# Moving one top-k block to ScalarE, the memory projections to fp32 matmuls, and w_out's splits to three engines, in a hybrid decoder layer

## The chip, the cores and the metric

The kernel runs on one core of a Trainium2 chip. The core has TensorE (PE in the profile, with its weight loads as PEld), VectorE (DVE), ScalarE (ACT), GpSimd (POOL) and SyncE (SP), which here only issues transfers. The metric is the device time of one execution in microseconds.

## The reference, cut to what matters

One decoder layer over 1024 tokens of width 1024. Group A is sparse attention: an indexer scores all keys, each query keeps its 256 best, and 8 heads attend to those. Group B is dense differential attention. Both go through `w_out`. Cross attention over 256 memory tokens and a convolutional gated feed-forward follow.

```python
def dsa_attention(q, k, v, q_idx, k_idx, w_idx):
    topk = min(TOPK_MAX, S // 4)                     # 256
    def block(args):                                 # 128 queries
        logits = jnp.einsum('bqhd,bsd->bqhs', qib, k_idx)
        score = jnp.einsum('bqh,bqhs->bqs', wib, jax.nn.relu(logits)).astype(jnp.float32)
        score = jnp.where(causal[None], score, -jnp.inf)
        _, idx = lax.top_k(score, topk)
        ...

def token_mixer(hn, cos, sin, w_in, ...):
    proj = hn @ w_in
    ...
    out_a = dsa_attention(q_a, k_a, v_a, q_i, k_i, w_i).reshape(B, S, A_WIDTH)
    out_b = diff_attention(q_b, k_b, v_b, lam)
    out_b = (rms_normalize(out_b) * (1.0 - lambda_init)).reshape(B, S, B_WIDTH)
    return jnp.concatenate([out_a, out_b], axis=-1) @ w_out

def cross_attention(hn, memn, w_xq, w_xk, w_xv, w_xo, g_xq, g_xk):
    q = rmsnorm((hn @ w_xq).reshape(B, S, X_HEADS, X_HEAD_DIM), g_xq)
    k = rmsnorm((memn @ w_xk).reshape(B, M, X_HEADS, X_HEAD_DIM), g_xk)
    v = (memn @ w_xv).reshape(B, M, X_HEADS, X_HEAD_DIM)
    ...

def reference(...):
    h = h + token_mixer(rmsnorm(h, g_mix), ...)
    h = h + cross_attention(rmsnorm(h, g_xattn), rmsnorm(mem, g_mem), ...)
    h = h + conv_glu(rmsnorm(h, g_ffn), ...)
```

## The kernel before

**Split products.** A float32 product is made of three matmuls in the format fp32r (`mm3`, lines 287 to 289): high times high, high times low, low times high. So each operand exists as a high part (a copy into fp32r) and a low part (the source minus the high part). Matmuls on plain float32 operands also occur: the transposes, the products with attention weights (`a_av`, line 1016, and `b_av`, line 776) and `x_o` (line 1255).

**Weights.** `Weights` holds a list of jobs in order of use. A job loads 128 x 2 x 512 floats into a `raw` tile (line 168, on SP's queue), and `parts` writes the high part (line 181 on ACT or line 183 on POOL) and the low part (line 184, on DVE or POOL) into `wp` pages, of which there are 12. A pair such as `("a", "d")` says which engine makes the high part and which the low part; `AD`, `PD`, `AP_` are such pairs. `pump` runs the next jobs when pages are free.

**Stages.** The projections from `w_in` come first (to about 270 us of the profile), then group B (270 to 470), then group A (470 to 690), then the rest of `w_out`, cross attention and the feed-forward. Beside group B, and at the start of group A, `mem_step` spreads the projections of the memory tokens (`mem_mm`: eight units of eight `mm3`, weights `w_xk` and `w_xv`, stationary side `memT`).

**Top-k.** For the query blocks 2 to 7 the threshold of each row is found bit by bit in 32 steps (`topk_iter`). Block i has 128 x (i+1) keys. `GROUPS` says on which engine a block counts. On ACT, a step is one `Sign` over the scores with a running sum (line 532) and then two short DVE instructions (lines 534 and 536) that set the next candidate, which the next Sign needs. On DVE, a step is one scan with a count per block (line 544) and two short ones (546 and 547, or 549 and 550). `topk_mask` makes the mask at the end. `tick` hands out steps according to `PACE`, one pair of numbers for each phase (projections, group B, group A): a step per that many microseconds of estimated work. `topk_finish` runs what is left before a block is used.

**Group A.** `a_qt` splits the queries (`split_heads`, lines 436 and 437) and transposes them, `a_s` makes the scores (lines 995 and 996) and adds the mask on DVE (998), `a_t` transposes (670) with copies on ACT (661), `a_av` multiplies by the values. `a_ob` normalizes group B's output (1027 to 1031). `wout_unit` makes the first half of the product with `w_out` inside this stage.

**Order.** The program is written unit by unit, and a scheduler then decides the order on each engine. Within an engine and within a queue, instructions keep that order.

Of the kernel before, what the change touches and what calls it, by code (L numbers as in the profile page):

```python
# [9 lines left out]
F32 = mybir.dt.float32  # L10
# [8 lines left out]
P = 128  # L19
# [25 lines left out]
def hybrid_layer(ctx, tc, I, out):  # L45
# [98 lines left out]
    class Weights:  # L144
# [9 lines left out]
        def load(self):  # L154

            while self.nload < len(self.jobs) and self.jobs[self.nload][1] is None:
                self.nload += 1
            if self.nload == len(self.jobs):
                return
            _, src, n, _, kind, _ = self.jobs[self.nload]  # L160
            raw = rawt()
            if kind == "memT":
                sp.dma_start(raw.rearrange("p a (b m) -> p a b m", b=2), src)
            elif self.nload == 0:
                for j in range(2):
# [20 lines left out]
        def split(self):  # L186
            i = self.nsplit
            key, src, n, engines, kind, _ = self.jobs[i]
            while src is not None and i not in self.raws:
                self.load()  # L190
# [25 lines left out]
            elif kind == "D":  # L216
                fpart(fi["g"][:, 1, :])
            elif kind == "memT":
                for j in range(2):
                    pg = self.page(key)  # L220
                    for b in range(2):
                        v = slice(256 * b, 256 * b + 256)
                        gk = gmem[:, n + 2 * j + b:n + 2 * j + b + 1]
                        act.activation(pg[:, 0, v], raw[:, j, v], AF.Copy, scale=gk)
                        dve.scalar_tensor_tensor(pg[:, 1, v], raw[:, j, v], gk, pg[:, 0, v].bitcast(F32),
                                                 op0=OP.mult, op1=OP.subtract)
            elif kind == "xq":
# [28 lines left out]

    def add_chunk(key, w, c0, n, engines):
        for k in range(0, KT, 2):
            W.add(key, w[k * P:(k + 2) * P, c0:c0 + n].rearrange("(j p) n -> p j n", p=P), n, engines)

    XW = 'CAAA'
    offs = np.cumsum([0] + W_CHUNKS)
# [3 lines left out]
    for k in range(0, KT, 4):  # L266
        W.add("memT", I["memT"][k * P:(k + 4) * P, :].rearrange("(a b p) m -> p a b m", a=2, p=P), k, None, "memT")
    for w in ("xk", "xv"):
        for c in range(2):
            add_chunk((w, c), I["w_" + w], 512 * c, 512, {"A": (AP_, ("p", "p")), "B": (AD, AP_), "C": (AD, AD), "D": (AD, PD), "E": (AP_, AP_)}[XW[2 * (w == "xv") + c]])  # L270
    for half in range(2):
        for c in range(2):
            add_chunk(("out", half, c), I["w_out"], 512 * c, 512, (PD, PD))
    for c in range(2):
# [157 lines left out]

    def split_heads(tag, src, nh):

        hl = rt(tag, [P, nh, 2, 64], F32R, "hl")
        act.copy(hl[:, :nh, 0, :], src)
        dve.tensor_tensor(hl[:, :nh, 1, :], src, hl[:, :nh, 0, :].bitcast(F32), op=OP.subtract)
        return hl
# [69 lines left out]

    GROUPS = [(x.split("-")[0], tuple(int(y) for y in x.split("-")[1])) for x in 'act-23,dve-45,dve-67'.split(",")]
    cand = [mtile([P, 3], I32, f"cand{g}") for g in range(len(GROUPS))]  # L510
# [85 lines left out]

    PACE = [dict(zip(("act", "dve"), [float(y) for y in x.split(",")])) for x in '4,6:4.5,10:4.5,5'.split(':')]
    phase = [0]
# [247 lines left out]
    def mem_prep():  # L846
        pages = W.get("memT", 4)
        for j in range(KT):
            v = pages[j // 2][:, :, (j % 2) * 256:(j % 2) * 256 + 256]
            mstat[j] = (v[:, 0, :], v[:, 1, :])  # L850
        for t in range(2):
# [10 lines left out]
    def mem_mm(key, t, p, ks):  # L862
        pages = W.get(key, 8)
        s = slice(t * P, (t + 1) * P)
        for k in ks:
            mh, ml = mstat[k]
            mm3(p, mh[:, s], ml[:, s], pages[k][:, 0, :], pages[k][:, 1, :], k == 0, k == KT - 1)

# [106 lines left out]
    def a_qt(i, g):  # L975
        if g == 0:
            a_qs[i] = kq([P, 8, P], F32R, "qas")
        hl = split_heads("hl", a_q[i][g], 4)
        p = trp()
# [44 lines left out]
    def a_ob(i):  # L1024
        r = small("rr")
        sq = rt("t2", [P, 512], F32, "sq")
        dve.tensor_tensor(sq, ob[i], ob[i], op=OP.mult)
        dve.tensor_reduce(ssb[:, i, :], sq.rearrange("p (h d) -> p h d", h=4), axis=AX.X, op=OP.add)
        rstd(pool, r[:, 0:4], ssb[:, i, :], 4, 1.0 / 128)
        pool.tensor_scalar(r[:, 0:4], r[:, 0:4], 1.0 - LAMBDA_INIT, 1.0, op0=OP.mult, op1=OP.mult)  # L1030
        dve.tensor_tensor(a_mix[i][:, 512:1024].rearrange("p (h d) -> p h d", h=4), ob[i].rearrange("p (h d) -> p h d", h=4),
                          r[:, 0:4].unsqueeze(2).to_broadcast([P, 4, P]), op=OP.mult)
# [683 lines left out]
```

## Time and profile before

| | |
|---|---|
| three runs | 1692.95, 1697.2 and 1699.25 us; median 1697.2 |
| the profiled execution | 1697.69 us, of which its span is 1695.9 |
| busy time in the span | PE 1570.8 us (93%), DVE 1296.0 (76%), ACT 736.7 (43%), POOL 666.8 (39%) |
| weight loads of PE | 1284.2 us (76%) |
| HBM | 129 GB/s over the span |

The 1.8 us between the profiled execution's time and its span lie outside the instructions. Shares over the whole span mix stages with different limits, so the stages are to be read one by one. A busy PE includes the tail of each matmul, which overlaps the next one, so that gaps shorter than the tail don't show as idle.

### The profile page before, as it was taken

Reading aid. Unit: us, or ns where it says so; the run is one execution under the profiler, and the core shown is the slowest. Engines: PE = TensorE matmul, PEld = TensorE weight load, DVE = VectorE, ACT = ScalarE, POOL = GpSimd, SP = SyncE. Lnnn points to the kernel's source line nnn. Section 1 sums busy time; section 2 is a strip of 40 time slices with the busy share of each in tenths; the row PEclk is TensorE's granted clock in tenths of the full one; section 3 lists DMA queues with packets and bytes.
Section 4 is the critical chain, followed back from the end, with each engine's and each line's share of the span. In section 5 each row is a group of like instructions: output and inputs, shape, how many; then the busy total and the mean of one; then the engine's idle time right before and its main releaser. Section 6 shows DMA issues by size and latency. Waiting matters only on the chain.

```text
span 1695.9 us, 22395 instructions
## 1 busy us (share of the span) xinstructions
PE 1570.8 (93%) x7660; PEld 1284.2 (76%) x7660; DVE 1296.0 (76%) x2524; ACT 736.7 (43%) x1469; POOL 666.8 (39%) x908
## 2 busy tenths in 40 slices
PE   8899988878889989999999978999999999899999
PEld 7788766667778778878777766887777777778887
DVE  5736998999999987467553588999988888665554
ACT  6545576566655326325442234333333333343432
POOL 2746666545440230140100032556666566541121
PEclk9999999899989999999999989999999999999999
DMA  8321225222230212261202121555544554698812
GB/s 284 94 82 58 71 93 163 73 62 78 90 100 26 70 68 69 71 220 63 75 25 88 62 87 65 179 174 191 174 164 166 179 180 167 251 366 320 315 50 75
DMA packets 112161, 220.05 MB, mean 130 GB/s; under 512 B 18480, under 2 KB 38448, under 8 KB 112048
## 3 DMA queue, kind: packets, MB, share of 16 engines
q1 hardware_dynamic: 91072, 148.37, 26.5%
q0 software_dynamic: 18384, 61.36, 10.3%
q10 hardware_dynamic: 2592, 8.91, 1.4%
q8 instruction: 60, 0.98, 0.2%
q14 instruction: 53, 0.43, 0.1%
HBM read 160.92 MB, written 57.67 MB: 129 GB/s over the span
## 4 chain that ended last, share of the span: by engine, by line
PE 47%; DVE 31%; DMA 8%; issue 6%; POOL 5%; ACT 3%; SPq 0%; ACTq 0%; DVEq 0%; POOLq 0%
PE acc L287 8%; PE acc L288 8%; PE acc L289 8%; DVE jk L544 6%; DVE wp L184 4%; PE big L288 3%; PE big L287 3%; PE big L289 3%; DMA fs<-u_d 2%; POOL fs L1529 2%; PE trp L287 2%; PE trp L288 2%; PE trp L289 2%; PE big L1255 2%; DMA raw<-in_w_ffn_in_dram 2%
## 5 line engine op out<-in xcount | busy, mean ns | idle before, releaser
L184 DVE TENSOR_TENSOR wp<-raw,wp 128x512 fp32r<-128x512 f32 (+1 forms) x200 | 192.9, 973 | 21.8 <-ACT wp L181 13.2
L181 ACT CAST wp<-raw 128x512 fp32r<-128x512 f32 (+1 forms) x188 | 110.1, 614 | 173.3 <-DVE raw L206 121.4
L1580 DVE TENSOR_TENSOR wp<-fo,wp 128x1024 fp32r<-128x1024 f32 x77 | 100.6, 1322 | 76.8 <-ACT wp L1579 75.2
L1529 POOL TENSOR_TENSOR fs<-fs,fs 128x512 f32<-128x512 f32 x88 | 126.8, 1441 | 77.6 <-DMA fs<-u_d 56.8
L1579 ACT CAST wp<-fo 128x1024 fp32r<-128x1024 f32 x77 | 79.8, 1049 | 108.9 <-PE big L289 47.0
L287 PE MATMUL acc<-wp,xh 128*128 128x512 f32 (+1 forms) x272 | 110.3, 407 | 9.4 <-ACT X L625 9.4
L183 POOL TENSOR_SCALAR wp<-raw 128x512 fp32r<-128x512 f32 (+1 forms) x64 | 46.7, 740 | 177.5 <-DVE rst L110 63.4
L289 PE MATMUL acc<-wp,xl 128*128 128x512 f32 (+1 forms) x272 | 109.8, 404 | 0.0
L288 PE MATMUL acc<-wp,xh 128*128 128x512 f32 (+1 forms) x272 | 109.5, 404 | 0.0
L661 ACT COPY pt<-trp 128x512 f32<-128x512 f32 (+3 forms) x144 | 65.6, 476 | 69.0 <-PE trp L670 68.5
L184 POOL TENSOR_TENSOR wp<-raw,wp 128x512 fp32r<-128x512 f32 x52 | 69.2, 1349 | 45.7 <-ACT wp L181 45.6
L1016 PEld LDWEIGHTS acc<-va_t,pt 128*128 128x128 f32 x576 | 74.0, 195 | 7.1 <-ACT pt L661 5.0
L1016 PE MATMUL acc<-va_t,pt 128*128 128x65 f32 x576 | 76.6, 273 | 2.6 <-ACT pt L661 2.0
L1626 POOL TENSOR_TENSOR hr<-hr,r 128x512 f32<-128x512 f32 x16 | 26.9, 1692 | 123.0 <-DMA fo<-ws_d 59.6
L1061 POOL DMA_DIRECT2D h_d<-xr x16 | 9.3, 579 | 165.6 <-DVE xr L1060 147.3
L999 ACT ACTIVATE ea<-ea,sta 128x128 f32<-128x128 f32 (+7 forms) x64 | 49.3, 777 | 49.8 <-DVE sta L998 46.4
L287 PEld LDWEIGHTS acc<-wp,xh 128*128 128x128 f32 x272 | 53.0, 195 | 23.0 <-ACT X L625 11.6
L544 DVE TENSOR_SCALAR_CACHE_REDUCE jk<-mb,cx 128x640 bf16<-128x640 uint16 (+1 forms) x64 | 68.6, 1072 | 0.7
L1482 POOL TENSOR_TENSOR fg<-fc,fg 128x1024 f32<-128x1024 f32 x21 | 50.9, 2425 | 36.3 <-ACT fc L1477 36.1
L544 DVE TENSOR_SCALAR_CACHE_REDUCE jk<-mb,cand 128x640 bf16<-128x640 bf16 (+3 forms) x60 | 64.4, 1073 | 0.4
L288 PE MATMUL acc<-wp,wp 128*128 128x512 f32 x152 | 61.2, 403 | 2.8 <-DVE wp L184 2.8
L1474 ACT ACTIVATE fc<-fa,cw 128x1024 f32<-128x1024 f32 x22 | 27.4, 1245 | 81.9 <-DVE fa L1433 72.2
(419 smaller groups left out, 5140.6 us busy)
## 6 DMA issues: line engine op xcount, KB each, us to landing
raw<-in_w_ffn_in_dram SPq DMA_DIRECT2D x44, 512.0 KB, 4.2
fs<-in_w_ffn_out_dram POOLq DMA_DIRECT2D x44, 256.0 KB, 3.8
ws_d<-fs POOLq DMA_DIRECT2D x44, 256.0 KB, 2.3
fs<-u_d POOLq DMA_DIRECT2D x44, 256.0 KB, 3.8
us_d<-fs POOLq DMA_DIRECT2D x44, 256.0 KB, 2.9
fo<-us_d SPq DMA_DIRECT2D x44, 256.0 KB, 5.3
fo<-ws_d SPq DMA_DIRECT2D x44, 256.0 KB, 5.4
u_d<-fg POOLq DMA_DIRECT2D x21, 512.0 KB, 4.4
```

The costliest lines, as they stand in the source:

```text
L181: act.copy(pg[:, 0, :n], src)
L184: (dve if el == "d" else pool).tensor_tensor(pg[:, 1, :n], src, pg[:, 0, :n].bitcast(F32), op=OP.subtract)
L287: pe.matmul(o, lhsT=lh, rhs=rh, start=start, stop=False)
L288: pe.matmul(o, lhsT=lh, rhs=rl, start=False, stop=False)
L289: pe.matmul(o, lhsT=ll, rhs=rh, start=False, stop=stop)
L544: dve.tensor_scalar(jk[:, :n], src, th[:, j:j + 1], None, op0=OP.is_ge, op1=OP.add, accum_out=cnt[:, j:j + 1])
L661: act.copy(dst, src)
L1016: pe.matmul(acc[:, hh * 65:hh * 65 + 65], lhsT=pt, rhs=va_t[:, kt, :], start=kt == 0, stop=kt == i)
L1482: pool.tensor_tensor(g, cv, g, op=OP.mult)
L1529: pool.tensor_tensor(o, p, q, op=op)
L1579: act.copy(hi, raw)
L1580: dve.tensor_tensor(lo, raw, hi.bitcast(F32), op=OP.subtract)
```

## The change

1. **Top-k.** Block 6 (896 keys) counts on ACT instead of DVE; block 7 stays on DVE alone. The paces become 7 and 12 in group B (from 4.5 and 10) and 4 and 4.5 in group A (from 4.5 and 5).
2. **Memory projections.** `memT` is stored once, scaled, as plain float32; `w_xk` and `w_xv` are loaded straight into a page ("direct"), with no split; each `mm3` becomes one float32 matmul. A chunk takes 4 pages instead of 8.
3. **w_out.** The first chunk's low parts are made on POOL (its high parts on POOL and ACT); in the other three chunks half of the high parts move from POOL to ACT, and the low parts stay on DVE.
4. **Group A.** The low part of the queries (line 437) and the scaling of group B's output (line 1031) move from DVE to POOL, the square (line 1027) from DVE to ACT.

```diff
@@ load / split
-            while self.nload < len(self.jobs) and self.jobs[self.nload][1] is None:
+            while self.nload < len(self.jobs) and (self.jobs[self.nload][1] is None or self.jobs[self.nload][4] == "direct"):
...
             elif kind == "memT":
+                pg = self.page(key).bitcast(F32)
                 for j in range(2):
-                    pg = self.page(key)
                     for b in range(2):
...
-                        act.activation(pg[:, 0, v], raw[:, j, v], AF.Copy, scale=gk)
-                        dve.scalar_tensor_tensor(pg[:, 1, v], raw[:, j, v], gk, pg[:, 0, v].bitcast(F32),
-                                                 op0=OP.mult, op1=OP.subtract)
+                        act.activation(pg[:, j, v], raw[:, j, v], AF.Copy, scale=gk)
+            elif kind == "direct":
+                sp.dma_start(self.page(key).bitcast(F32), src)
@@ jobs
-    XW = 'CAAA'
...
-            add_chunk((w, c), I["w_" + w], 512 * c, 512, {"A": (AP_, ("p", "p")), "B": (AD, AP_), "C": (AD, AD), "D": (AD, PD), "E": (AP_, AP_)}[XW[2 * (w == "xv") + c]])
+            add_chunk((w, c), I["w_" + w], 512 * c, 512, None, "direct", 1)
...
-            add_chunk(("out", half, c), I["w_out"], 512 * c, 512, (PD, PD))
+            add_chunk(("out", half, c), I["w_out"], 512 * c, 512, (("p", "p"), AP_) if half + c == 0 else (PD, AD))
@@ top-k
-    GROUPS = [(x.split("-")[0], tuple(int(y) for y in x.split("-")[1])) for x in 'act-23,dve-45,dve-67'.split(",")]
+    GROUPS = [(x.split("-")[0], tuple(int(y) for y in x.split("-")[1])) for x in 'act-23,act-6,dve-45,dve-7'.split(",")]
-    PACE = [dict(zip(("act", "dve"), [float(y) for y in x.split(",")])) for x in '4,6:4.5,10:4.5,5'.split(':')]
+    PACE = [dict(zip(("act", "dve"), [float(y) for y in x.split(",")])) for x in '4,6:7,12:4,4.5'.split(':')]
@@ mem_mm
-        pages = W.get(key, 8)
+        pages = W.get(key, 4)
...
-            mh, ml = mstat[k]
-            mm3(p, mh[:, s], ml[:, s], pages[k][:, 0, :], pages[k][:, 1, :], k == 0, k == KT - 1)
+            pe.matmul(p, lhsT=mstat[k][:, s], rhs=pages[k // 2].bitcast(F32)[:, k % 2, :], start=k == 0, stop=k == KT - 1)
@@ a_qt, a_ob
-        hl = split_heads("hl", a_q[i][g], 4)
+        hl = split_heads("hl", a_q[i][g], 4, pool)
...
-        dve.tensor_tensor(sq, ob[i], ob[i], op=OP.mult)
+        act.activation(sq, ob[i], AF.Square)
...
-        dve.tensor_tensor(a_mix[i][:, 512:1024].rearrange("p (h d) -> p h d", h=4), ob[i].rearrange("p (h d) -> p h d", h=4),
+        pool.tensor_tensor(a_mix[i][:, 512:1024].rearrange("p (h d) -> p h d", h=4), ob[i].rearrange("p (h d) -> p h d", h=4),
```

Three places show how rows move. The first is ACT's order early in group B, before the change: `e` are the exponentials of group B, `pt` and `qbs` the copies that PE's next matmuls read.

```order
347 L889 COPY kt_3310<-trp_3305 128x512
348 L876 ACTIVATE sq_3315<-X_3313 128x512
349 L755 ACTIVATE e_3377,st_3371<-e_3377,st_3371 128x256 x2
350 L777 ACTIVATE ob_2733<-acc_3143,st_3166 128x128
351 L727 CAST qbs_3363<-trp_3360 128x256
352 L661 COPY pt_3369<-trp_3365 128x384
353 L727 CAST qbs_3435<-trp_3432 128x256
354 L755 ACTIVATE e_3462,st_3451<-e_3462,st_3451 128x896
```

The same place with the change (the line numbers are those of the changed file, one to three lower); `mb_940` is the Sign of block 6, and `cand_522` the candidate that it waits for.

```order
333 L531 ACTIVATE mb_940,ccnt_526<-sc_941,cand_522 128x896
334 L754 ACTIVATE e_3331,st_3325<-e_3331,st_3325 128x256
335 L886 COPY kt_3264<-trp_3259 128x512
336 L873 ACTIVATE sq_3269<-X_3267 128x512
337 L754 ACTIVATE e_3331,st_3325<-e_3331,st_3325 128x256
338 L776 ACTIVATE ob_2719<-acc_3097,st_3120 128x128
339 L726 CAST qbs_3317<-trp_3314 128x256
340 L531 ACTIVATE mb_940,ccnt_526<-sc_941,cand_522 128x896
341 L660 COPY pt_3323<-trp_3319 128x384
342 L726 CAST qbs_3357<-trp_3354 128x256
343 L754 ACTIVATE e_3384,st_3373<-e_3384,st_3373 128x896
```

A Sign now stands among group B's copies about once a unit: 22 of its 32 steps lie beside group B and 10 beside group A.

The second place is DVE's order early in group A (block 2), before the change: `jk` are the scans of the blocks 6 (128x896) and 7 (128x1024), `ea` the masked scores.

```order
950 L546 TENSOR_SCALAR crej_529<-ccnt_526 128x2
951 L1031 TENSOR_TENSOR mixt_5274<-ob_2731,rr_5405 128x512
952 L547 SCALAR_TENSOR_TENSOR cand_523<-crej_529,cand_523 128x2
953 L1020 RECIPROCAL sta_5232<-acc_5275 128x4
954 L544 TENSOR_SCALAR jk_5241,ccnt_526<-mb_936,cand_523 128x896
955 L1021 TENSOR_TENSOR mixt_5274<-acc_5275,sta_5232 128x256
956 L437 TENSOR_TENSOR hl_5559<-qat_5494,hl_5559 128x4x64
957 L544 TENSOR_SCALAR jk_5243,ccnt_526<-mb_938,cand_523 128x1024
```

The same place with the change:

```order
942 L543 TENSOR_SCALAR jk_5090,ccnt_528<-mb_942,cand_524 128x1024
943 L995 ISA ea_5103,sta_5063<-big_5100,mb_932,ra 128x384
944 L995 ISA sta_5063 128x1
945 L545 TENSOR_SCALAR crej_532<-ccnt_528 128x1
946 L533 TENSOR_SCALAR crej_530<-ccnt_526 128x1
947 L546 SCALAR_TENSOR_TENSOR cand_524<-crej_532,cand_524 128x1
948 L535 SCALAR_TENSOR_TENSOR cand_522<-crej_530,cand_522 128x1
949 L995 ISA ea_5133,sta_5063<-big_5130,mb_932,ra 128x384
```

The scans of block 6 and the rows of lines 1031 and 437 are gone from DVE; two short rows a step (533 and 535) stay behind for block 6. Of the 32 scans of block 6, 4 stood beside group B and 28 beside group A; of block 7's, 4 and 28 before, 1 and 31 now.

The third place is SP's queue just ahead of group B, before the change: `qa_d` are stores of the last projection, `raw` weight loads, `vb` and `mtok` what group B and the memory norm read first.

```order
82 L654 DMA qa_d<-X_2483 128x512
83 L654 DMA qa_d<-X_2542 128x512
84 L168 DMA raw_2682<-in_w_xk_dram 128x2x512
85 L691 DMA vb_2741<-vb_d 128x8x128
86 L853 DMA mtok_2743<-in_mem_dram 128x1024
87 L853 DMA mtok_2747<-in_mem_dram 128x1024
88 L168 DMA raw_2788<-in_w_xk_dram 128x2x512
```

With the change:

```order
87 L226 DMA wp_2879<-in_w_xk_dram 128x2x512
88 L653 DMA qa_d<-X_2540 128x512
89 L226 DMA wp_2955<-in_w_xk_dram 128x2x512
90 L226 DMA wp_3033<-in_w_xk_dram 128x2x512
91 L226 DMA wp_3095<-in_w_xk_dram 128x2x512
92 L226 DMA wp_3157<-in_w_xv_dram 128x2x512
93 L690 DMA vb_2727<-vb_d 128x8x128
94 L851 DMA mtok_2729<-in_mem_dram 128x1024
```

Between the store of `qa_d` and `vb` four weight loads of 512 KB now stand where one stood. A direct load writes into a page, so it waits for the last matmul that read the page before.

## Rows read from the trace of the kernel before

**Rows 1.** Busy time by stage (PE, PEld, DVE, ACT, POOL), granted clock, DMA share, GB/s.

```profile
165.00:270.00 105.00, 95.58 (x399) 75.45 (x398) 100.33 (x284) 71.51 (x173) 69.13 (x105) 0.97 0.24 80
270.00:470.00 200.00, 161.56 (x940) 134.75 (x938) 190.51 (x469) 125.82 (x310) 103.18 (x171) 0.93 0.31 95
470.00:690.00 220.00, 199.08 (x1316) 174.06 (x1316) 193.76 (x442) 106.30 (x202) 42.14 (x114) 0.97 0.21 68
650.00:690.00 40.00, 38.99 (x308) 36.54 (x307) 21.93 (x40) 28.37 (x43) 0.00 (x0) 1.00 0.14 47
270.00:300.00 30.00, 22.96 (x104) 16.42 (x103) 28.96 (x70) 20.17 (x45) 19.69 (x43) 0.89 0.67 207
```

**Rows 2.** Chain that ended last, by line, in 270 to 470, then 470 to 690.

```profile
by line: DVE e L753 12.6%; DVE e L765 9.9%; DVE jk L544 8.0%; PE acc L776 7.6%; issue 5.4%; ACT e L755 4.2%; DVE st L764 3.5%; PE acc L287 2.8%; PE acc L288 2.7%; DVE wp L184 2.7%; PE acc L289 2.7%; DVE sc L584 2.5%; DVE kb L705 2.5%; PE tr
by line: DVE jk L544 25.0%; DVE ea L998 11.5%; PE acc L1016 8.5%; issue 8.3%; PE trp L670 5.1%; DVE wp L184 5.0%; PE big L995 2.6%; DVE mx L1042 2.5%; PE big L996 2.3%; DVE sc L584 1.9%; DMA h_d<-xr 1.8%; DVE hl L437 1.8%; DVE xr L1060 1.7%
```

**Rows 3.** PE's timeline: start, length, line; two stretches, in cross attention.

```profile
821.12 3.59 PE L1255 MATMUL big<-ptx,vx 128*128 128x512 f32 x8
824.55 0.60 PE L1245 MATMUL trp<-ident,ex 128*128 128x128 f32 x4
...
949.75 0.39 PE L287 MATMUL acc<-wp,oxh 128*128 128x512 f32 x1
...
950.43 0.39 PE L287 MATMUL acc<-wp,oxh 128*128 128x512 f32 x1
```

**Rows 4.** DVE's groups in 270 to 470: count, busy us, mean ns, idle before.

```profile
L184 DVE TENSOR_TENSOR wp<-raw,wp 128x512 fp32r<-128x512 f32 x8 | 6.4, 817 | 0.0
L544 DVE TENSOR_SCALAR_CACHE_REDUCE jk<-mb,cand 128x896 bf16<-128x896 bf16 x3 | 3.4, 1140 | 0.0
L764 DVE SCALAR_TENSOR_TENSOR st<-st,neglam 128x1 f32<-128x1 f32 x32 | 10.8, 344 | 0.2
```

**Rows 5.** Line 764 over the span: shortest, median and longest ns.

```profile
L764 DVE SCALAR_TENSOR_TENSOR st<-st,neglam x32: 196/217/1337, 291.0 to 463.2; 128x1 f32<-128x1 f32 x32
```

**Rows 6.** DVE's groups in 470 to 690, shapes apart where they differ.

```profile
L544 DVE TENSOR_SCALAR_CACHE_REDUCE jk<-mb,cx 128x1024 bf16<-128x1024 uint16 x16 | 20.4, 1275 | 0.3
L544 DVE TENSOR_SCALAR_CACHE_REDUCE jk<-mb,cx 128x896 bf16<-128x896 uint16 x16 | 18.2, 1139 | 0.3
L184 DVE TENSOR_TENSOR wp<-raw,wp 128x512 fp32r<-128x512 f32 x28 | 20.0, 739 | 0.8 <-POOL wp L183 0.8
L437 DVE TENSOR_TENSOR hl<-qat,hl 128x256 fp32r<-128x256 f32 x14 | 5.8, 419 | 0.0
L1031 DVE TENSOR_TENSOR mixt<-ob,rr 128x512 f32<-128x512 f32 x8 | 5.5, 690 | 0.0
L546 DVE TENSOR_SCALAR crej<-ccnt 128x2 int32<-128x2 f32 x13 | 2.5, 196 | 0.1
L547 DVE SCALAR_TENSOR_TENSOR cand<-crej,cand 128x2 int32<-128x2 int32 x13 | 2.0, 156 | 0.1
L544 DVE DVE_READ_ACCUMULATOR jk<-mb,cx 128x1 f32 x32 | 2.6, 82 | 0.0
```

**Rows 7.** ACT in group B: two rows of its timeline, and its splits in 270 to 470.

```profile
296.37 1.05 ACT L755 ACTIVATE e<-e,st 128x896 f32<-128x896 f32 x1 [1.40 <-DVE st L753]
...
297.41 0.36 ACT L727 CAST qbs<-trp 128x256 fp32r<-128x256 f32 x1
...
L181 ACT CAST wp<-raw 128x512 fp32r<-128x512 f32 x17 | 10.2, 618 | 7.8 <-DMA raw<-in_w_xk_dram 4.1 <-DMA raw<-in_w_xv_dram 1.7 <-POOL wp L184 0.8
```

**Rows 8.** What the Signs of the blocks 2 and 3 (line 532) waited for: us, times.

```profile
  DVE cand L536: 24.3, 18
```

**Rows 9.** POOL's low parts in 270 to 470.

```profile
L184 POOL TENSOR_TENSOR wp<-raw,wp 128x512 fp32r<-128x512 f32 x24 | 32.5, 1369 | 5.1 <-ACT wp L181 5.0
```

**Rows 10.** Waits: PE in 470 to 690, POOL in 270 to 470: us, times, longest.

```profile
PE big L995 <- DVE sta L998: 7.4, 10, 1.1
...
POOL hl L717 <- DMA qt<-qk_d: 3.9, 2, 2.6
```

More of the change, by code (lines that the diff above doesn't have):

```diff
@@ L188, in split @@
             key, src, n, engines, kind, _ = self.jobs[i]
-            while src is not None and i not in self.raws:
+            while src is not None and kind != "direct" and i not in self.raws:
                 self.load()
@@ L255, in hybrid_layer, with add_chunk @@
     W = Weights()
-    def add_chunk(key, w, c0, n, engines):
+    def add_chunk(key, w, c0, n, engines, kind="std", npages=2):
         for k in range(0, KT, 2):
-            W.add(key, w[k * P:(k + 2) * P, c0:c0 + n].rearrange("(j p) n -> p j n", p=P), n, engines)
-    XW = 'CAAA'
+            W.add(key, w[k * P:(k + 2) * P, c0:c0 + n].rearrange("(j p) n -> p j n", p=P), n, engines, kind, npages)
     offs = np.cumsum([0] + W_CHUNKS)
@@ L266, in hybrid_layer @@
     for k in range(0, KT, 4):
-        W.add("memT", I["memT"][k * P:(k + 4) * P, :].rearrange("(a b p) m -> p a b m", a=2, p=P), k, None, "memT")
+        W.add("memT", I["memT"][k * P:(k + 4) * P, :].rearrange("(a b p) m -> p a b m", a=2, p=P), k, None, "memT", 1)
     for w in ("xk", "xv"):
         for c in range(2):
-            add_chunk((w, c), I["w_" + w], 512 * c, 512, {"A": (AP_, ("p", "p")), "B": (AD, AP_), "C": (AD, AD), "D": (AD, PD), "E": (AP_, AP_)}[XW[2 * (w == "xv") + c]])
+            add_chunk((w, c), I["w_" + w], 512 * c, 512, None, "direct", 1)
     for half in range(2):
         for c in range(2):
-            add_chunk(("out", half, c), I["w_out"], 512 * c, 512, (PD, PD))
+            add_chunk(("out", half, c), I["w_out"], 512 * c, 512, (("p", "p"), AP_) if half + c == 0 else (PD, AD))
     for c in range(2):
@@ L431, in rope, with split_heads @@
         dve.tensor_tensor(x, x, ctab, op=OP.mult)
-    def split_heads(tag, src, nh):
+    def split_heads(tag, src, nh, eng=None):
         hl = rt(tag, [P, nh, 2, 64], F32R, "hl")
         act.copy(hl[:, :nh, 0, :], src)
-        dve.tensor_tensor(hl[:, :nh, 1, :], src, hl[:, :nh, 0, :].bitcast(F32), op=OP.subtract)
+        (eng or dve).tensor_tensor(hl[:, :nh, 1, :], src, hl[:, :nh, 0, :].bitcast(F32), op=OP.subtract)
         return hl
@@ L846, in mem_prep @@
     def mem_prep():
-        pages = W.get("memT", 4)
+        pages = W.get("memT", 2)
         for j in range(KT):
-            v = pages[j // 2][:, :, (j % 2) * 256:(j % 2) * 256 + 256]
-            mstat[j] = (v[:, 0, :], v[:, 1, :])
+            mstat[j] = pages[j // 4].bitcast(F32)[:, j % 4 // 2, (j % 2) * 256:(j % 2) * 256 + 256]
         for t in range(2):
@@ L916, in mem_unit @@
         if t == 1:
-            W.free(8)
+            W.free(4)
             if (w_, c) == ("xv", 1):
-                W.free(4)
+                W.free(2)
         if w_ == "xk":
```

## The prediction

> **What bounds the kernel now.** I read busy time by stage first, since shares over the whole span hide which engine limits where [rows 1]. Beside group B (270 to 470 us) DVE is busy 190.5 of 200 us, beside group A (470 to 690) 193.8 of 220; PE is busy 161.6 and 199.1. At the end of group A (650 to 690), where top-k is over, DVE falls to 21.9 of 40 us and PE rises to 39.0 of 40, at full clock. The reader is to see there that the same group A work runs on a full PE as soon as DVE has room. The chain of waits says the same [rows 2]: beside group A the top-k scans (line 544) alone hold 25.0% of it (55 us), the masked scores on DVE (998) 11.5%, the splits (184) 5.0%; PE's lines that are shown hold less than a fifth. Beside group B the chain is spread over DVE, PE and ACT: the DVE lines shown add up to 41.7%, the memory projections (287 to 289) to 8.2%, ACT's exponentials to 4.2%. The waits of PE show how DVE holds it in group A: the next scores wait for the mask addition 7.4 us, in 10 pieces [rows 10]. So a microsecond off DVE is worth most beside group A, and about half of one beside group B.
>
> **The memory projections.** Two float32 operands as wide as these are multiplied in `x_o`: eight records of line 1255 start at 821.12 and the next instruction at 824.55, so 0.429 us each [rows 3], and a float32 matmul is two records (32 in the program, 64 in the trace). One costs 0.858 us. An `mm3` takes 950.43 - 949.75 = 0.68 us in the same rows. Each of the 64 products costs PE 0.178 us more, 11.4 us in all. By the changed order 8 lie ahead of group B, 48 beside it, 8 beside group A: 1.4, 8.5 and 1.4 us.
>
> What goes: eight DVE splits of `memT` ahead of group B, half as wide as the rows of line 184, so at most 0.8 us each; eight of `w_xk` at 0.817 us = 6.4 us beside group B [rows 4]; on POOL 24 low parts, 32.5 us [rows 9]; on ACT 14 of 17 copies (three of w_out's remain), 14 x 0.618 = 8.7 us [rows 7]. Line 184 holds 2.7% of group B's chain, 5.4 us, so nearly all of those splits counts [rows 2].
>
> **Top-k.** A scan of block 6 costs DVE 1.139 + 0.082 us (the count is read by a second row), one of block 7 1.275 + 0.082 [rows 6]. Beside group A 28 scans of block 6 go and 3 of block 7 come: 34.2 - 4.1 = 30.1 us saved. Beside group B 4 and 3 go: 9.0 us. Each step of block 6 leaves DVE two short instructions, as wide as lines 546 and 547 or narrower: 0.196 + 0.156 = 0.352 us. Ten beside group A cost 3.5 us; 22 beside group B 7.7, with 15 as the upper bound if each is as long as the mean of line 764 there, 0.344 [rows 4]. ACT gets 32 Signs of 896 columns. An exponential of that width starts 1.04 us before the next row [rows 7], and I take that price: 22.9 us beside group B, 10.4 beside group A. The last mask steps change by two instructions and are left out.
>
> **w_out and group A.** Eight low parts leave DVE, at the price of group A's 0.739 us: 5.9 us. The query splits save 14 x 0.419 = 5.8, the scaling 8 x 0.690 = 5.5, the squares the same price, six of eight beside group A, 4.1 [rows 6]. What POOL gains there (16 query splits, 8 scalings) lies in the 178 us in which it is idle [rows 1], and ACT's copies and squares in its 114 idle us. If that cover failed, the query splits would stall PE's transposes of the next block; they are issued half a block ahead, so I price this at nothing.
>
> **Beside group A.** DVE saves 30.1 + 5.9 + 5.8 + 5.5 + 4.1 - 3.5 = 48 us and needs 146 of the 220. PE needs 199.1 + 1.4 = 200.5 and becomes the bound. At the density of 650 to 690 (97.5%) that is 205.6 us: **14 us saved**. The low end is 7, if PE gets to 94% only (213 us). [...]
>
> **Beside group B.** The splits give 5.4 us. The rest of DVE's saving is 9.0 for scans and about 3 for their short rows, two query splits and two squares, less 7.7 for block 6's short rows: 4.6 us net. DVE's lines hold 41.7% of the chain and DVE is busy 95% of the time, so 0.44 of that counts: 2.0. PE's 8.5 us more count by how much of the 50 `mm3` that the order has there (34 us) is on the chain, 8.2% of 200 = 16.4 us, so 0.48: 4.1 lost. ACT gets 22.9 - 8.7 = 14.2 us more; its exponentials hold 4.2% of the chain (8.4 us) at 125.8 busy, so 0.07 of that counts: 1 lost.
>
> Then POOL. Line 764 works on one column; its median is 0.217 us and its longest 1.337 [rows 5], its mean 0.344 [rows 4]. Its 32 runs lose 4.1 us to something that lasts about as long as a POOL instruction (1.369 us, rows 9). With 24 low parts gone from POOL and eight of w_out's come, POOL does 21.5 us less of its 103, a fifth: I take 1 us off group B's chain. [...]
>
> Net: 5.4 + 2.0 - 4.1 - 1 + 1 = **3 us saved**. The bounds are a gain of 12 (PE's extra hidden, DVE's counting in full) and a loss of 10: three more loads of 512 KB stand ahead of `vb`, `mtok` and the query loads on SP. At the 207 GB/s of 270 to 300 [rows 1] they take 7.6 us, and POOL already waits 3.9 us for queries [rows 10].
>
> **Ahead of group B** DVE is busy 100.3 of 105 us and PE idle 9.4 [rows 1]; without eight splits I take 1 us, bounds 0 and 4. Behind group A everything is as it was: PE is the bound, and the splits of later weights start no later.
>
> **Sum.** 14 + 3 + 1 = 18 us. The profiled execution took 1697.69 us (span 1695.9 and 1.8 around it), 0.5 over the median of 1697.2. So 1679 us.
>
> **Rivals.** [...]
>
> *Nothing to see.* Another wait comes up where DVE's goes: PE stays at 94% beside group A (7), group B loses 5 to the later loads and the longer matmuls, and nothing is won ahead: 1695. For it speaks that the chain of group B changes engine all the time and that PE's waits for the mask addition are short, 1.1 us at most [rows 2, 10], so that an edit may only show the next wait.
>
> *Slower: ACT's queue becomes what group B waits for.* The Signs of the blocks 2 and 3 left ACT waiting 24.3 us for the candidate from DVE [rows 8], 0.76 us for each of 32 steps. In the changed order a Sign stands ahead of copies that PE needs, about one a unit. If each of the 22 holds them up by its length and such a wait, that is 22 x 1.80 = 39.6 us, less the 8.7 of copies gone: 31 lost beside group B, 14 won beside group A, so 1714. It decides from about 18 of these 31 us on. Against it speaks that ACT is idle 74 of 200 us there, and that a step only comes every 7 us of estimated work, long enough for DVE's answer. [...]
>
> **How the numbers follow.** My forecast (1669 to 1688) gets 0.45, the larger gain 0.24, no change 0.19, slower 0.12. Half a per cent (8.5 us) is about what a measurement of this kernel tells from no change: faster than 1688.7 has 0.71, within 0.18, slower 0.11. The range, 1657 to 1703, leaves out the slow rival and the far end of the large gain, some 0.1 each.
>
> **What would show it.** Right: beside group A PE is busy over 95%, DVE about 70%, line 544 falls to some 43 us and leaves the head of the chain, and the stage takes about 206 us. Beside group B the stage takes 195 to 199 us, with a float32 matmul at 0.43 us a record. Wrong: exponentials, copies or PE's transposes that wait for line 531 or for ACT behind it; PE waiting for page loads at 270 to 290; or a group A that is still held by the mask addition with DVE below 75%, which would mean that the length of the path from scores to copies, not DVE's load, was the limit.

## The result

| | changed kernel | kernel before | ratio |
|---|---|---|---|
| first measurement | 1683.24 us, median of 4 (1679.49 to 1688.28) | 1695.08, median of 4 (1691.88 to 1699.25) | 0.9931 (95%: 0.9906 to 0.9955) |
| repeated beside the first experiments | 1690.05, median of 12 (1682.49 to 1696.78) | 1693.96, median of 23 (1687.40 to 1700.47) | 0.9973 (0.9954 to 0.9993) |

The forecast was 1679, the range 1657 to 1703. Faster, but by how much depends on which runs one has: the mean of all 17 runs of the changed kernel is 1688.0 us, of all 65 of the kernel before 1694.6, so 6.5 us or 0.4%, less than the half per cent that was called no change. Three profiles of each kernel show where it lies. The stages are cut at the starts of PE's rows: the last projection matmul, the last values product of group B (line 775), that of group A (1013), the first and the last piece of the feed-forward stretch, the last matmul.

| us, three profiles each | before | changed | mean difference |
|---|---|---|---|
| up to the last projection matmul | 270.3, 270.2, 270.9 | 270.2, 269.7, 270.1 | -0.5 |
| group B | 198.7, 198.1, 199.3 | 212.8, 208.4, 212.0 | **+12.4** |
| group A | 237.8, 242.2, 240.1 | 228.4, 228.4, 228.1 | **-11.7** |
| w_out to the start of feed-forward | 329.7, 332.7, 330.5 | 329.6, 330.2, 330.2 | -1.0 |
| feed-forward | 436.1, 430.2, 426.5 | 426.2, 425.1, 430.4 | -3.7 |
| last stage | 218.8, 217.4, 218.7 | 215.0, 215.1, 214.9 | -3.3 |

Group B gave back all that group A won. Of the 8 us that are left in these profiles, 7 lie in the last two stages, where the code is the same in both kernels.

Two rows of the changed kernel's PE timeline are the cuts of group A:

```profile
482.98 0.88 PE L775 MATMUL acc<-vb,pt 128*128 128x128 f32 x6
...
711.40 1.00 PE L1013 MATMUL acc<-va_t,pt 128*128 128x65 f32 x8
```

Busy time by stage of the changed kernel (columns as in [rows 1]; group B now ends at 483, group A at 712):

```profile
165.00:270.00 105.00, 95.99 (x391) 75.92 (x390) 97.35 (x275) 68.32 (x165) 67.39 (x105) 0.93 0.29 95
270.00:300.00 30.00, 17.63 (x65) 11.61 (x64) 23.27 (x60) 13.48 (x31) 17.55 (x39) 0.78 0.80 252
270.00:483.00 213.00, 168.66 (x882) 126.86 (x880) 169.65 (x483) 139.63 (x341) 71.55 (x147) 0.91 0.29 89
483.00:712.00 229.00, 216.32 (x1430) 188.78 (x1429) 161.29 (x400) 130.75 (x246) 49.29 (x121) 0.97 0.19 62
```

Beside group A DVE falls to 70% and PE stands at 94%. Beside group B DVE falls from 95% to 80%, yet the stage is longer: no engine there is full. Its chain, and that of group A, answer to [rows 2]:

```profile
by line: PE acc L864 13.0%; PE acc L775 8.9%; DVE e L752 8.6%; ACT e L754 7.5%; issue 5.2%; DMA mtok<-in_mem_dram 4.6%; PE big L745 4.4%; PE big L744 4.3%; PE trp L669 4.1%; ACT mb L531 3.0%; DVE e L764 3.0%; PE trp L701 2.8%; DVE sc L583 2
by line: PE acc L1013 18.3%; PE trp L669 9.3%; DVE ea L995 7.6%; PE acc L286 7.0%; PE acc L288 6.8%; PE acc L287 6.8%; DVE jk L543 4.9%; issue 4.8%; PE big L992 4.7%; PE big L993 4.3%; PE trp L978 2.9%; DVE wp L184 2.3%; PE trp L1037 2.3%; 
```

The scans (now line 543) went from 25.0% of group A's chain to 4.9%; PE heads it. They answer to [rows 6] with these two groups (DVE, 483 to 712):

```profile
L543 DVE TENSOR_SCALAR_CACHE_REDUCE jk<-mb,cx 128x1024 bf16<-128x1024 uint16 x16 | 20.4, 1275 | 0.1
L543 DVE TENSOR_SCALAR_CACHE_REDUCE jk<-mb,cand 128x1024 bf16<-128x1024 bf16 x15 | 19.1, 1276 | 0.2
```

In group B's chain two things are new: the Signs of line 531, and mem's rows (`mtok`), whose load comes late. ACT's Signs there and what they wait for:

```profile
L531 ACT ACTIVATE mb<-sc,cand 128x896 bf16<-128x896 f32 x22 | 22.9, 1041 | 7.4 <-DVE cand L535 6.4 <-DVE st L762 1.1
```

One of the 22, in ACT's timeline (start, length, line), then PE's over the same microseconds:

```profile
351.15 1.04 ACT L754 ACTIVATE e<-e,st 128x896 f32<-128x896 f32 x1 [0.20 <-DVE st L752]
352.10 0.19 ACT L754 ACTIVATION_READ_ACCUMULATOR e<-e,st 128x1 f32 x1
352.19 0.35 ACT L776 ACTIVATE ob<-acc,st 128x128 f32<-128x128 f32 x1
352.44 1.03 ACT L531 ACTIVATE mb<-sc,cand 128x896 bf16<-128x896 f32 x1
353.38 0.19 ACT L531 ACTIVATION_READ_ACCUMULATOR mb<-sc,cand 128x1 f32 x1
353.47 1.05 ACT L660 COPY pt<-trp 128x512 f32<-128x512 f32 x2
```

```profile
349.51 1.04 PE L669 MATMUL trp<-ident,e 128*128 128x128 f32 x8
...
354.09 1.26 PE L775 MATMUL acc<-vb,pt 128*128 128x128 f32 x8 [3.15 <-ACT pt L660]
```

The transposes are done at 350.55. Their copies start only at 353.47, behind an exponential, an output copy and the Sign; PE waits 3.15 us. 1.03 of that is the Sign, which nothing in group B needs. It is the longest of PE's waits for ACT there. In two places such a wait is followed by a lower clock (windows of the same kernel, columns as above; in the second pair PE waits 3.33 us for line 704 on DVE, the low part of the keys, not for ACT):

```profile
350.00:354.00 4.00, 0.94 (x9) 0.80 (x7) 3.56 (x12) 3.80 (x9) 0.00 (x0) 1.00 0.46 132
354.00:358.00 4.00, 3.91 (x21) 3.56 (x22) 4.00 (x16) 2.94 (x11) 0.77 (x2) 0.63 0.03 8
...
370.00:374.00 4.00, 0.78 (x4) 0.78 (x5) 3.90 (x13) 2.99 (x9) 3.02 (x6) 0.76 0.43 127
374.00:378.00 4.00, 4.00 (x19) 3.90 (x18) 4.00 (x16) 1.92 (x5) 0.00 (x0) 0.50 0.22 61
```

PE is busy for 0.94 and 0.78 us of 4, and in the 4 us after that the granted clock is 0.63 and 0.50. A score matmul of 384 columns, whose row is 0.34 us long at 348.49, takes 0.52 at 375.20.

### The profile page after: what moved, and what is told of

It reads as the page before. It is cut to its first block, busy times and chain, and to the rows that moved or that the text cites. A ratio compares the mean times of both kernels' runs of the same rounds, so it can differ in the third digit from the quotient of the medians.

```text
span 1686.5 us, 22216 instructions
## 1 busy us (share of the span) xinstructions
PE 1576.2 (93%) x7596; PEld 1277.5 (76%) x7596; DVE 1229.9 (73%) x2468; ACT 769.7 (46%) x1536; POOL 639.8 (38%) x888
## 4 chain that ended last, share of the span: by engine, by line
PE 49%; DVE 27%; DMA 8%; issue 6%; ACT 5%; POOL 3%; SPq 0%; ACTq 0%; DVEq 0%; POOLq 0%
PE acc L286 8%; PE acc L288 8%; PE acc L287 8%; DVE wp L184 5%; DMA raw<-in_w_ffn_in_dram 3%; PE acc L1013 3%; DVE fc L1473 2%; PE big L287 2%; PE big L288 2%; PE big L286 2%; DVE fc L1472 2%; PE trp L669 2%; PE acc L864 2%; PE big L1252 2%; DVE jk L543 1%
## 5 line engine op out<-in xcount | busy, mean ns | idle before, releaser
L184 DVE TENSOR_TENSOR wp<-raw,wp 128x512 fp32r<-128x512 f32 (+1 forms) x184 | 181.3, 996 | 28.3 <-ACT wp L181 17.9
L1577 DVE TENSOR_TENSOR wp<-fo,wp 128x1024 fp32r<-128x1024 f32 x77 | 101.8, 1338 | 76.0 <-ACT wp L1576 71.3
L531 ACT ACTIVATE mb<-sc,cand 128x384 bf16<-128x384 f32 (+1 forms) x96 | 75.4, 786 | 38.3 <-DVE cand L535 33.9
L183 POOL TENSOR_SCALAR wp<-raw 128x512 fp32r<-128x512 f32 (+1 forms) x36 | 24.6, 691 | 177.2 <-DVE rst L110 63.5
L286 PEld LDWEIGHTS acc<-wp,xh 128*128 128x128 f32 x272 | 53.2, 196 | 22.2 <-ACT X L624 10.8
L995 DVE CUSTOM_DVE_ANT_0 ea<-big,mb,ra 128x384 f32<-128x384 f32 (+5 forms) x48 | 45.3, 945 | 27.7 <-PE trp L669 24.6
L184 POOL TENSOR_TENSOR wp<-raw,wp 128x512 fp32r<-128x512 f32 x36 | 47.5, 1334 | 42.5 <-ACT wp L181 42.2
L752 DVE CUSTOM_DVE_ANT_0 e<-big,tri,rqk 128x1024 f32<-128x1024 f32 (+7 forms) x64 | 50.3, 810 | 18.2 <-PE big L745 13.8
L287 PEld LDWEIGHTS acc<-wp,xh 128*128 128x128 f32 x272 | 53.3, 196 | 11.5
L1474 ACT ACTIVATE fc<-fc 128x1024 f32<-128x1024 f32 x22 | 23.4, 1062 | 84.5 <-DVE fc L1473 84.5
```

The lines of the kernel that those rows point to most:

```text
L184: (dve if el == "d" else pool).tensor_tensor(pg[:, 1, :n], src, pg[:, 0, :n].bitcast(F32), op=OP.subtract)
L286: pe.matmul(o, lhsT=lh, rhs=rh, start=start, stop=False)
L287: pe.matmul(o, lhsT=lh, rhs=rl, start=False, stop=False)
L531: act.activation(mb[i], sc[i], AF.Sign, bias=cf[:, j:j + 1], scale=-1.0, accum_out=cnt[:, j:j + 1])
L1577: dve.tensor_tensor(lo, raw, hi.bitcast(F32), op=OP.subtract)
```

## The experiments

Three theories, by name. Loads: group A's gain is real, and group B lost it to the loads that now stand ahead of `mtok` and the queries on SP; this came first. Signs: group B lost it to the Signs in ACT's queue. Chance: the difference in the feed-forward stretch is that of single executions. The expectations number theirs afresh: "theory 1" is the loads in e3 (in e4 DVE's relief beside group A, in e6 that the moves cost group B nothing) and, after these two had run, the Signs in e5, e7 and e8; "theory 2" is chance in e1 and the loads in e8. The first row is the changed kernel's mean of three profiles; group B and group A are cut as above, "first" is the time, counted from the last projection matmul, of the 25th score matmul of group B. The stages of e3 to e10 are from one profile each, and each ratio is to runs of the kernel before that were taken beside it.

| | group B | group A | "first" | time, runs | ratio to before (95%) |
|---|---|---|---|---|---|
| changed kernel | 211.1 | 228.3 | 38.6 to 39.5 | 1690.05, 12 | 0.9973 (0.9954 to 0.9993) |
| e3, memory projections alone | 194.3 | 236.8 | 37.1 | 1680.94, 4 | 0.9921 (0.9903 to 0.9938) |
| e4, top-k alone | 203.7 | 233.3 | 29.7 | 1690.72, 12 | 0.9978 (0.9964 to 0.9992) |
| e5, all but top-k | 193.2 | 232.0 | 36.8 | 1678.85, 6 | 0.9899 (0.9875 to 0.9923) |
| e6, w_out and group A's moves alone | 198.1 | 232.4 | 29.6 | 1682.43, 6 | 0.9929 (0.9906 to 0.9951) |
| e7, half the Signs beside group B | 200.2 | 238.2 | 39.4 | 1685.71, 8 | 0.9943 (0.9922 to 0.9963) |
| e8, mem's norm earlier | 208.7 | 228.1 | 44.2 | 1689.84, 12 | 0.9970 (0.9950 to 0.9990) |
| e9, e5 with loads on ACT's queue | 197.7 | 233.0 | 39.8 | 1684.27, 5 | 0.9940 (0.9924 to 0.9956) |
| e10, changed, loads on ACT's queue | 211.8 | 228.4 | 41.1 | 1692.24, 12 | 0.9996 (0.9979 to 1.0014) |

The kernel before has 198.7, 240.0 and 29.7 to 29.8 in these columns (means of three for the stages). The 194.7 that e5's expectation gives for e3 cuts the same row of PE 0.4 us later.

**e1, e2, e11, e12: the two kernels again, no edit.**

> The changed kernel a second time. In the first pair of profiles group B became 14 us longer (last values product of B at 469.6 before, 483.6 after), group A 9 us shorter (237.9 to 228.5 us from there to the last values product of A), and the feed-forward stretch, whose order is the same in both kernels, 10 us shorter (435.7 to 425.8 us from its first product to the last accumulation). Theory 1, the change moves all three: this profile shows the same three numbers within 3 us. Theory 2, the feed-forward difference is chance of one execution: it lies elsewhere between 425 and 436 us here, and group B and A repeat. Time ratio 0.993 by both, with a narrower interval.

> The kernel before a second time, for a second profile. If the feed-forward stretch of 435.7 us is the kernel's own, it is 434 to 437 us again. If it is chance, it may come out near 426 us, and then the 10 us that the changed kernel gained there are no effect of the change. Group B's end at 469 us and group A's 238 us should repeat within 3 us by both theories.

> A third profile of the kernel before. The feed-forward stretch was 436.1 and 430.2 us in the first two, and 425.1 to 432.2 in eight profiles of changed kernels, with the same code. If it is chance there, this one lies anywhere between 425 and 436; if the kernel before is slower there by itself, 430 or more again. Group B 198 to 199 and group A 238 to 242.

> A third profile of the changed kernel. The feed-forward stretch was 426.2 and 425.1 us in the first two. If it is chance, anything between 425 and 436; if the change shortens it, 427 or less again. Group B 208 to 213, group A 228 to 229.

Groups B and A repeat within 5 us; the ratio came out at 0.997, not at the expected 0.993. The feed-forward stretch doesn't: it was 436.1, 430.2 and 426.5 us in the kernel before, 425.1 to 432.2 in eleven profiles of changed kernels. Its rows in the first and third profile of the kernel before (one fence each, columns as in [rows 1]):

```profile
1036.50:1472.70 436.20, 422.14 (x1789) 334.30 (x1788) 386.26 (x427) 143.07 (x217) 256.68 (x275) 1.00 0.51 174
```

```profile
1041.00:1467.50 426.50, 419.64 (x1788) 334.06 (x1787) 375.15 (x426) 142.78 (x216) 259.26 (x275) 1.00 0.52 177
```

PE's work is the same within 2.5 us; DVE's differs by 11.1, and the longest of PE's waits there are for DVE. So the 10 us that the first pair of profiles showed there are chance. The last stage's 3.3 us are not settled: PE's wait for the last gate values from DVE at its start is 6.9, 5.5 and 6.8 us before, 3.7 in all three of the changed kernel, 3.3 and 3.9 in e10 and e7, but 7.4 in e8, which has all of the change. No experiment was aimed at it.

**e3: the memory projections alone.**

```diff
+            add_chunk((w, c), I["w_" + w], 512 * c, 512, None, "direct", 1)
...
+            pe.matmul(p, lhsT=mstat[k][:, s], rhs=pages[k // 2].bitcast(F32)[:, k % 2, :], start=k == 0, stop=k == KT - 1)
```

> The kernel before with the memory projections alone changed (float32 matmuls, pages loaded directly). Theory 1, the loads that now stand ahead of mem's token rows and the queries delay group B's start: group B ends 8 to 14 us later than 469.6, PE's transposes wait about 9 us for POOL near 285 to 293 us, and the kernel is 5 to 10 us slower than before, near 1702. Rival, the Signs on ScalarE stretch group B: here there are none beyond those of before, group B ends within 3 us of 469.6 and the time is within 4 us of 1695 (5 us of splits saved, 4 to 8 us of longer matmuls lost).

Both were wrong: group B became 4 us shorter and the kernel 13 us faster. The late start that the load theory rests on is there (PE waits 7.9 us for the query split, "first" is 7 us late), but by the 57th score matmul this version stands at 65.5 us where the kernel before stands at 68.0. What makes up for it seems to be mostly DVE: 83 forms of DVE instruction occur as often in group B of both kernels, and together they take 198.3 us before and 182.0 here. Nearly all of that is in the 33 forms that work on two tensors (`TENSOR_TENSOR` and `SCALAR_TENSOR_TENSOR`): 86.2 to 71.3 us, against 112.0 to 110.8 in the other 50. Two of the 33 before (groups over 270 to 470):

```profile
L765 DVE SCALAR_TENSOR_TENSOR e<-e,st,e 128x1024 f32<-128x1024 f32 x4 | 6.1, 1526 | 0.1
L882 DVE SCALAR_TENSOR_TENSOR X<-X,rr,gkq 128x256 f32<-128x256 f32 x8 | 5.7, 757 | 0.1
```

and in e3 (270 to 464), with line 763, which answers to 764 in [rows 4], and the busy time of the stretch:

```profile
L763 DVE SCALAR_TENSOR_TENSOR st<-st,neglam 128x1 f32<-128x1 f32 x32 | 7.5, 236 | 0.4
L764 DVE SCALAR_TENSOR_TENSOR e<-e,st,e 128x1024 f32<-128x1024 f32 x4 | 5.1, 1285 | 0.1
L879 DVE SCALAR_TENSOR_TENSOR X<-X,rr,gkq 128x256 f32<-128x256 f32 x8 | 3.9, 526 | 0.0
...
270.00:464.00 194.00, 161.24 (x878) 119.88 (x877) 173.59 (x464) 115.95 (x292) 64.50 (x140) 0.95 0.30 94
```

POOL has 39 us less to do there (103.2 to 64.5). The other versions agree: where POOL keeps its work beside group B (e4, e6), such two-tensor forms keep their time (90.4 and 91.8 us, 88.2 and 88.3); where it has 72 us (e5, the changed kernel), they fall from 84.0 to 73.3 and from 81.8 to 69.7. No run changes POOL's work alone, and how much of the 4 us comes from it is not shown.

**e4: top-k alone; e5: all but top-k.** One edit, added to the kernel before or taken out of the changed one:

```diff
-... 'act-23,dve-45,dve-67'        '4,6:4.5,10:4.5,5'
+... 'act-23,act-6,dve-45,dve-7'   '4,6:7,12:4,4.5'
```

> The kernel before with the top-k schedule alone changed (block 6 on ScalarE, the pace of the steps). Theory 1, VectorE's relief beside group A is the gain: group A becomes 7 to 10 us shorter (228 to 231 us), group B stays within 4 us of 187 us (first scores to last values product), time 1685 to 1690. Rival, the Signs of 896 columns hold up ScalarE's copies beside group B: group B becomes 8 us or more longer, group A 8 us shorter, and the time stays within 4 us of 1695.

> The changed kernel with the top-k schedule of before (memory projections, w_out and group A's moves stay). Theory 1, the 22 Signs of block 6 on ScalarE are what makes group B longer, and only together with the shorter memory projections, which leave ScalarE more of the path: group B (last projection matmul to last values product) falls from 208 to 213 us to 193 to 198, as with the memory projections alone (194.7). Group A keeps the relief of the other edits (21 of the 48 us off VectorE) and takes 230 to 235 us. Time about 1675 to 1680, faster than the changed kernel. Rival, what lengthens group B is the other edits (squares and high parts on ScalarE, splits on GpSimd): group B stays above 204 us, and the time above 1685.

Added to the kernel before, the top-k edit makes group B 5.0 us longer and group A 6.7 shorter: between theory and rival. Taken out of the changed kernel it gives group B back 17.9 us and costs group A 3.7: e5 came out as its theory 1 said. It has the lowest ratio of all, 1.0% under the kernel before (its interval overlaps those of e3 and e6), and is faster than the changed kernel. In e5's group B the same PE instructions take 159.7 us at a mean clock of 0.96:

```profile
270.00:463.80 193.80, 159.68 (x882) 117.66 (x881) 172.77 (x457) 118.29 (x297) 72.00 (x146) 0.96 0.31 97
```

In the changed kernel they take 168.7 at 0.91 (x882 both): 9 of the 19.6 us between these two profiles are PE's own work at the lower clock, the rest waits. Little of that is put down to ACT directly: PE's waits for ACT in group B come to 17.6 us in e5 and 20.3 in the changed kernel, those for DVE to 8.8 and 15.2. The largest step is one line (e5, then the changed kernel; us, times, longest):

```profile
PE trp L669 <- DVE kb L704: 2.2, 2, 1.3
```

```profile
PE trp L669 <- DVE kb L704: 9.4, 5, 3.3
```

DVE in turn waits 9.2 us for ACT there in e5 and 19.7 in the changed kernel. So a delay in ACT's queue reaches PE mostly by way of DVE.

Why the same 22 Signs cost 5 us in the kernel before and 17.9 in the changed one is settled only in part. The traces show where the difference lies: in e4 PE's own work grows by 2.3 us (161.1 to 163.4, clock 0.93 to 0.92) and in the changed kernel by 9.0, from a clock that stood at 0.96; and DVE's waits for ACT grow by 2.0 us in e4 (5.4 to 7.4) against 10.5. DVE is busy 93% of group B in e4 and 80% in the changed kernel, so that ACT's delays may have lain behind DVE's; that is argued, no run tests it. In group B the parts do not add up: e3, e6 and e4 alone are 4.4 and 0.6 us shorter and 5.0 longer, together nothing, where the whole change is 12.4 longer.

**e6: w_out and group A's moves alone.**

```diff
-            add_chunk(("out", half, c), I["w_out"], 512 * c, 512, (PD, PD))
+            add_chunk(("out", half, c), I["w_out"], 512 * c, 512, (("p", "p"), AP_) if half + c == 0 else (PD, AD))
...
-        hl = split_heads("hl", a_q[i][g], 4)
+        hl = split_heads("hl", a_q[i][g], 4, pool)
```

> The kernel before with w_out's low parts and group A's moves alone. Theory 1: group B is that of before within 3 us (198.4), group A about 4 us shorter than the 238 to 242 of before, time 1687 to 1692. Rival, these edits load ScalarE and GpSimd beside group B: group B 205 or more, time 1695 or more.

Group B is unchanged, group A 7.6 us shorter where 4 were expected, and the time of 1682.43 us lies below the 1687 to 1692 expected: what moved to POOL and ACT was covered.

**e7: fewer Signs beside group B.**

```diff
-    ... '4,6:7,12:4,4.5'
+    ... '4,6:14,12:4,4.5'
```

> The changed kernel with one number altered: beside group B a ScalarE step every 14 us of estimated work in place of 7, so that about half of block 6's Signs go from group B to group A. Theory 1, each Sign beside group B costs about its length: group B falls by about half of what it lost, to 200 to 206 us, and group A stays at 228 to 231 us, since ScalarE has room there; time 1680 to 1684. Rival, the number of Signs there is not the cause: group B stays at 208 to 213, or group A gives back what B gains, and the time stays at 1687 to 1690.

9 Signs are left beside group B, which takes 200.2 us; with 22 it takes 211.1, with none (e5) 193.2. That is 0.78 to 0.84 us for each. But group A is 238.2 with 23 of them, 228.3 with 10, so 0.76 us for each there too, against the expected "ScalarE has room there". DVE is as busy in both (162.0 and 161.3 us), and PE's waits for the copies `pt` grow from 3.9 to 8.4 us. The time, 1685.71, is above the 1680 to 1684 expected. Its rows:

```profile
466.80:704.90 238.10, 220.30 (x1428) 191.91 (x1427) 161.99 (x425) 143.59 (x274) 51.93 (x122) 0.95 0.18 59
...
L531 ACT ACTIVATE mb<-sc,cand 128x896 bf16<-128x896 f32 x23 | 23.9, 1037 | 3.6 <-DVE cand L535 3.6
```

ACT is idle for 94 of these 238 us, and the Signs cost all the same.

**e8: mem's norm ahead of the loads; e9, e10: the late loads on another queue.**

```diff
# e8: in the last projection chunk, in place of mem_prep
+            if c == 4 and t < 2:
+                sp.dma_start(xt.rearrange("p a b -> p (a b)"), I["mem"][t * P:(t + 1) * P, :])
+                act.activation(jk, xt.rearrange("p a b -> p (a b)"), AF.Square, accum_out=ssm[:, t:t + 1])
# e9 (on e5), e10 (on the changed kernel)
-        sp.dma_start(qt...          sp.dma_start(xt, I["mem"]...
+        (act if 2 <= u < 6 else sp).dma_start(qt...          act.dma_start(xt, I["mem"]...
```

> The changed kernel with the sums of squares of mem's rows moved ahead of the direct loads, into the last projection chunk, so that no GpSimd work beside group B waits for the late load of those rows. Theory 2, the late load is what group B lost: PE's wait of 8.9 us for the query split (284 to 293 us) goes, and group B becomes 8 us shorter, 200 to 205, time 1679 to 1682. Theory 1, the gap at the start is made up for by the 64th score product anyway, as it is with the memory projections alone, and ScalarE's Signs take what comes later: group B becomes less than 4 us shorter, time 1684 to 1688.

> The version of the fifth run (changed kernel, top-k schedule of before) with mem's two row loads and four of the first query loads issued from ScalarE's queue in place of SyncE's, where they stand behind a weight load that waits for PE to free its page. Theory, what is late at group B's start is what stands behind that load: PE's wait of 7.5 us for the query split there falls below 3 us, the 24th score product comes 4 to 7 us earlier than 36.8 us after the last projection, and since group B made up for the gap by its 64th product before, its end gains only 0 to 4 us: 190 to 194 us, time 1675 to 1679. Rival, ScalarE's own queue now waits for the loads: group B 196 or more, time 1682 or more.

> The changed kernel with the same loads on ScalarE's queue. If the late loads are a part of the 10 to 14 us that group B lost beside the Signs, group B falls from 208 to 213 to 200 to 204 us and the time by 5 to 8 us. If the Signs are nearly all of it, group B stays above 205 and the time within 3 us of the changed kernel's.

None of the three made group B start earlier; its first score matmul came 3 to 5 us later (14.8, 13.9 and 15.2 us after the projections, 10.6 without the edits). In e8 PE's wait for the query split fell from 8.9 to 2.3 us, but waits of 3.6, 2.5 and 4.5 us for DVE and ACT stand in its place. e9 came out as its rival said (197.7, 1684.27), and e10 as it said for Signs alone (211.8, 1692.24). What stands ahead on SP is a weight load that holds the queue. SP's queue in e5 (start, length, line):

```profile
274.04 2.88 SPq L851 DMA_DIRECT2D mtok<-in_mem_dram  x2
276.96 0.43 SPq L690 DMA_DIRECT2D vb<-vb_d  x1
277.44 4.24 SPq L226 DMA_DIRECT2D wp<-in_w_xv_dram  x1
281.79 0.44 SPq L653 DMA_DIRECT2D qa_d<-X  x1
282.33 0.38 SPq L709 DMA_DIRECT2D qt<-qk_d  x1
```

Stores and queries stand behind it, not only `mtok`. The load of `wp` takes 4.24 us where the others of its kind take 0.5. e9's expectation has it wait for PE to free its page; the profile doesn't show that (line 226's waits for PE come to 0.7 us from 262 to 300), and what it waits for stays open. Its cost was not taken away by any version here. But e3 and e5 make up for the late start and end group B 4 to 6 us ahead of the kernel before, and in the changed kernel itself the 57th of the 192 score matmuls comes 65.7 to 70.4 us after the projections, in the kernel before 67.6 to 68.0. At most 2.8 of the 12.4 us are lost by then. The load theory falls, that of the Signs stands.

## Why the prediction came out as it did

- **Group A, 14 saved: right.** 11.7 measured, above the low end of 7. DVE's scans fell by 29.4 us, from 68.9 to 39.5 (30.1 forecast), and DVE is at 70%. PE got to 94%, not 95 or more, and the granted clock stayed at 0.97: the low end's condition, with a gain above its 7. That PE is what holds the stage now fits the parts: alone they save 7.6 (e6), 6.7 (e4) and 3.2 us (e3), together 11.7, not 17.5.
- **Group B, 3 saved: wrong, 12.4 lost,** outside the bounds of 12 and -10. The step that failed is ACT's: "its exponentials hold 4.2% of the chain (8.4 us) at 125.8 busy, so 0.07 of that counts: 1 lost". In this kernel a Sign costs 0.76 to 0.84 us in group B and in group A alike (e5, e7), 17.9 beside group B in all, about half of it as a lower clock of PE (0.96 in e5, 0.91 in the changed kernel), which the sum had no term for. In the kernel before the same Signs cost 5.0 (e4). The share of an engine's *old* instructions on the chain (4.2%) said nothing here of a new one that stands ahead of them in its queue. The rival "ACT's queue becomes what group B waits for" had the mechanism right in the main, with 31 lost where 17.9 were; it was given 0.12. Its waits of 0.76 us a Sign were too long: 7.4 us for 22. In the rows at 352.44 the copies of transposes that were done at 350.55 start only behind the Sign, at 353.47.
- **POOL's relief, 1 saved: too small.** POOL did 31.6 us less beside group B in the changed kernel, where 21.5 were forecast, and 38.7 less in e3, where the same DVE instructions took 16.3 us less and the mean of line 764 fell from 344 to 236 ns. Its median stayed (217 and 219), its longest run fell from 1337 to 559 ns (360 in the changed kernel). So the median, which I went by, was the wrong guide: the forms that got shorter work on two tensors (86.2 to 71.3 us in e3), and the mask addition (line 752), which has neither of the two forms, kept its length (1280 and 1281 ns for 1024 columns). Why these and not the others, no run shows. What POOL's relief brought in time is not shown by itself: the memory projections as a whole were forecast at 5.4 - 4.1 + 1 = 2.3 saved beside group B and saved 4.4 (e3).
- **The larger gain, given 0.24: shown by no run.** The granted clock stayed at 0.97 beside group A and went from 0.93 to 0.91 beside group B, and the fastest version (e5) has a median of 1678.85 us.
- **The longer matmuls: right.** 16 records of line 864 take 7.03 us in the changed kernel's PE timeline, 0.44 each, and e3 is the faster for the exchange.
- **The bound of 10 for the late loads** has its mechanism in the trace (a wait of 8.9 us at 284), but the stage makes up for it.
- **Ahead of group B 1, behind group A 0:** 0.5 measured, and 8 us behind group A that I hadn't, of which 3.7 can't be told from chance and 3.3 have no cause that a run shows.

So it was luck that 1679 came near the first runs: group B was 15 us off, 8 us came from behind group A without a cause, and the median of those four runs lies 7 us below that of the twelve after them. By its own steps, with group B at +12.4 in place of -3, the forecast would have been 1694.

## What to carry to other kernels

Work that is put into the queue of an engine that takes part in a chain from engine to engine can cost most of its length at each place, idle time on that engine or not (0.76 to 0.84 us of 1.04 here, 0.23 net in e4, where DVE was busy 93%); price it by what stands behind it in the queue, not by the engine's share of the chain. Before moving work off a full engine, ask which of the moves relieves it without entering another's chain: here dropping a split altogether (e3) and moving pieces to POOL half a block ahead (e6) paid, while moving a count into ACT's queue brought 0.2% alone (e4) and cost 0.7% on top of the others (e5). And compare stage by stage over several profiles: one stage of the same code differed by 10 us from one execution to the next, more than the whole effect.

## What the runs showed of the hardware that I had not expected

- DVE instructions on two tensors got shorter by 17% over a stage (86.2 to 71.3 us) when GpSimd had 38% less work there, with nothing changed in them; the others hardly changed (112.0 to 110.8).
- Behind two PE waits of about 3 us (3.15 and 3.33) the granted clock was 0.63 and 0.50 in the next 4 us, where it was 0.91 over group B.
- A stage with PE and DVE both near full (feed-forward, PE 97 to 98%, DVE 88 to 89%) varied between 425 and 436 us with PE's instructions in the same order.
